# Keeping both split parts of three in four trunk weight tiles in DRAM

## The chip, the cores and the metric

The kernel runs on one core of a Trainium2 chip. The metric is the device time in microseconds (us) of one execution. Before the change the median of three runs is 1823.28 us (1819.3 to 1824.56). Five engines work side by side, each through its own list of instructions in order: TensorE (PE) for matrix products, VectorE (DVE), ScalarE (ACT) and GpSimd (POOL) for elementwise work, SyncE (SP), which here issues nearly all transfers between DRAM and the on-chip memory. They wait for each other through semaphores.

## The reference

One layer of a streaming encoder in float32, over 1024 prompt frames and 32 sample frames (1056 columns), width 1024. Shortened:

```
h = rms_norm(x, g_mix);  z = h @ w_in            # q k v, conv_h conv_B conv_C, two gates
a = window_attention(q, k, v) @ w_attn_out
bo = (cb * causal_conv3(cc * ch)) @ w_conv_out
x = x + (sigmoid(ga) * a + sigmoid(gb) * bo) @ w_mix_out
hc = rms_norm(x, g_cross)
x = x + memory_attention(hc @ w_cq) @ w_co
hm = rms_norm(x, g_mlp)
x = x + square(relu(hm @ w_up)) @ w_down
y = rms_norm(x, g_final)
```

`w_conv_out` and `w_mix_out` (called `w_mix` in the kernel) are 1024 x 1024, `w_cq` is 1024 x 256, `w_co` 256 x 1024, `w_up` 1024 x 4096.

## The kernel before

**Layout.** Activations lie transposed: 128 features on the partitions, frames along the columns. The 1056 columns are cut into three chunks of 384, 384 and 288. Features come in 8 blocks of 128. Each weight is cut into tiles of 128 x 1024 float32 (0.524 MB); such a tile makes one block of 128 outputs from 8 blocks of inputs (a tile of `w_co` makes four blocks from two).

**Split products.** To keep float32 accuracy with the faster matmul type, each operand is split into a rounded high part and a low part, the remainder. `gemm` (lines 170 to 177) runs three matmuls for each of 8 blocks: high x high (line 175), high weight x low activation (176), low weight x high activation (177): 24 matmuls a tile and chunk. The split of a weight tile is a cast on ACT (`wh<-wr`, line 119) and a subtraction on DVE (`wl<-wr,wh`, line 120).

**The order of weights.** `item` collects steps into a list, and `worder` the weight tiles that they need in this order. `next_w` keeps up to three tiles ready ahead (`LOOK = 2`). `issue_w` makes one ready: it fetches the raw tile into `wr` (two buffers, line 137), takes a high and a low buffer (`wh`, `wl`, three each), and splits. The buffers rotate, so a tile's high and low parts can be written only when TensorE has left the tile that was three before.

**Kept tiles.** The trunk runs once for each chunk: eight tiles of `w_conv_out` (`do_conv_out`), then eight of `w_mix` (`do_mix`). Cross-attention of a chunk (`cross_steps`: two tiles of `w_cq`, the scores and values, two of `w_co`) runs beside the trunk of the next chunk, one step after each trunk tile (`beside`). Cross-attention of chunk three runs beside the first eight tiles of `w_up` for chunks one and two; these eight then serve chunk three. So 28 tiles are used three times each. `kept` names those tiles (line 1274): the odd ones, 14 of 28. When such a tile is first used, its low part is stored to DRAM (line 154); in its two further uses the raw tile and the low part are loaded (lines 137 and 148) and only the cast is done (line 149). The other 14 are fetched and split at each use.

**Beside the tiles.** `do_conv_out` loads `t1` (line 786) and multiplies by a gate (line 790); line 791 adds on POOL. `do_mix` loads the input rows (line 801), adds them on DVE (line 805), and splits the scaled result (lines 255, 256). Cross-attention copies and adds its two halves (lines 918, 919), and splits (925 to 931) for `do_co` (943 to 945), whose result DVE adds in line 947. Lines 972 to 976 normalise rows for the up products, store them (973) and split them. Line 816 loads memory keys, line 828 splits memory values. Three accumulators (`acc`) rotate, so an addition on DVE that is late holds back TensorE.

**Order.** The program text gives dependencies and a rough order; a planner with a model of each engine's time lays down each engine's list before the run. SP's list is one of these: a load that waits for a buffer holds back all that SP issues behind it.

Of the kernel before, what the change touches and what calls it, by code (L numbers as in the profile page):

```python
# [10 lines left out]
F32 = mybir.dt.float32  # L11
# [7 lines left out]
P = 128  # L19
# [19 lines left out]
def hybrid_step(ctx: ExitStack, tc: tile.TileContext, io):  # L39
    nc = tc.nc  # L40
    act, dve, pool_e, pe, sp = nc.scalar, nc.vector, nc.gpsimd, nc.tensor, nc.sync
# [3 lines left out]
    def nm(s):  # L45
        uid[0] += 1
        return f"{s}_{uid[0]}"
# [15 lines left out]
    dram = ctx.enter_context(tc.tile_pool(name="dram", bufs=1, space=DRAM))  # L63
# [42 lines left out]
    plan, worder, kept = [], [], {}  # L106
# [11 lines left out]
    def split(hi, lo, src):  # L118
        act.copy(hi, src)  # L119
        dve.tensor_sub(lo, src, hi.bitcast(F32))  # L120

    def weight(key):
        name, *at = key
        if name in ("w_down", "w_sum"):
            q, j, t = at
            return (wsum_d if name == "w_sum" else io[name])[j, t, :, :, q].rearrange("i p c -> p i c")
        src = io[name]
        for j in at:
            src = src[j]
        return src  # L130

    fetched = []

    def fetch_w():
        raw = wp.tile([P, 1024], F32, tag="wr", bufs=2, name=nm("wr"))
        src = weight(worder[wpos[0] + len(fetched)])
        sp.dma_start(raw.rearrange("p (i c) -> p i c", i=4) if len(src.shape) == 3 else raw, src)
        fetched.append(raw)

    def issue_w():  # L140
        if not fetched:
            fetch_w()
        raw = fetched.pop(0)
        key = worder[wpos[0]]
        hi = wp.tile([P, 1024], F32R, tag="wh", name=nm("wh"))
        lo = wp.tile([P, 1024], F32R, tag="wl", name=nm("wl"))
        if kept.get(key) is not None:
            sp.dma_start(lo.bitcast(F32), kept[key])
            act.copy(hi, raw)
        else:  # L150
            split(hi, lo, raw)
            if key in kept:
                kept[key] = dram.tile([P, 1024], F32, name=nm("wl_d"))
                sp.dma_start(kept[key], lo.bitcast(F32))
        ready.append((worder[wpos[0]], (hi, lo)))
        wpos[0] += 1

    def next_w(key):
        while len(ready) <= LOOK and wpos[0] < len(worder) and worder[wpos[0]] is not STOP:
            issue_w()  # L160
        k, w = ready.pop(0)
        assert k == key, (k, key)
        return w
# [104 lines left out]
    def norm_x():  # L268
# [48 lines left out]
        with tc.manual_schedule(engines={mybir.EngineType.SP}):  # L317
            load_x()
        parts(0, range(1))
        issue_w()  # L320
        parts(0, range(1, NF))
        issue_w()
        issue_w()
        wk, wv = ready[0][1], (ready[1][1], ready[2][1])
# [91 lines left out]
    def do_K(pr, extras=()):  # L416
        def fn(w):
            kt = at_tile([P, NT], F32, "kt")
            ktt[pr] = kt
            for c, (o, n) in enumerate(CH):  # L420
                a = acc_tile([P, n])
                gemm(a, w, xg[c])
                dve.tensor_mul(kt[:, o : o + n], a, R[c])
                after(extras, c)
            sp.dma_start(io["o_k"][pr], kt[:, 896:])

        return fn
# [22 lines left out]
    def do_Q(kv, j, extras=()):  # L450
        def fn(w):
            for c, (o, n) in enumerate(CH):
                npr = min(n, NPR - o)
                if j == 0:
                    qs[kv, c] = at_tile([P, 4, npr], F32R, "QA" if c < 2 else "QB", 2 if c < 2 else 1)
                    if n > npr:
                        qs[kv, 3] = at_tile([P, 4, n - npr], F32R, "QC")
                a = acc_tile([P, n])
                gemm(a, w, xg[c])
                t = tmp(n)  # L460
                dve.scalar_tensor_tensor(t, a, 0.125, R[c], op0=ALU.mult, op1=ALU.mult)
                parts = [(qs[kv, c], slice(0, npr))]
                if n > npr:
                    parts.append((qs[kv, 3], slice(npr, n)))
                for q, s in parts:
                    for e in range(2):
                        own, other = slice(64 * e, 64 * e + 64), slice(64 - 64 * e, 128 - 64 * e)
                        h = 2 * j + e
                        act.copy(q[own, h], t[own, s])
                        dve.tensor_sub(q[other, h], t[own, s], q[own, h].bitcast(F32))  # L470
                after(extras, c)

        return fn
# [151 lines left out]
    def do_gate(f, extras=()):  # L625
        def fn(w):
            for c, (o, n) in enumerate(CH):
                a = acc_tile([P, n])
                gemm(a, w, xg[c])
                t = gate_slot(c, f)  # L630
                dve.tensor_mul(t, a, R[c])
                act.activation(t, t, AF.Sigmoid)
                sg[c][f] = t
                after(extras, c)

        return fn
# [21 lines left out]
    for i, h in enumerate(hosts):  # L658
# [9 lines left out]
        if h[0] == "Q":  # L668
            fn, key = do_Q(h[1], h[2], extras), qt(h[1], h[2])
        elif h[0] == "K":  # L670
            fn, key = do_K(h[1], extras), ("w_in", 8 + h[1])
        elif h[0] == "G":
            fn, key = do_gate(h[1], extras), ("w_in", 34 + h[1])
        else:
            fn, key = do_conv(*h, extras), conv_w(h[1], h[0])
# [577 lines left out]
    def beside(steps, fillers, late=()):  # L1253
        for i, filler in enumerate(fillers):
            item(*filler)
            for x in [x for at, x in late if at == i]:
                item(lambda x=x: x())
            if steps:
                kind, what = steps.pop(0)
                for x in what:  # L1260
                    if kind == "items":
                        item(*x)
                    else:
                        item(lambda x=x: x())
        return steps

    def trunk(c):
        return [(do_conv_out(c, f), ("w_conv_out", f)) for f in range(NF)] + [
            (do_mix(c, f), ("w_mix", f)) for f in range(NF)
        ]  # L1270

    up0 = lambda c: [do_up(j, c) for j in range(NF)]
    for name, n in (("w_conv_out", NF), ("w_mix", NF), ("w_cq", 2), ("w_co", 2), ("w_up", NF)):
        kept.update(((name, j), None) for j in range(1, n, 2))
    left = beside([], trunk(0))
    left = beside(cross_steps(0), trunk(1))

# [322 lines left out]
```

## Time and profile before

| | before |
|---|---|
| median of runs | 1823.28 us |
| profiled execution, its own time | 1822.32 us |
| its span, first to last instruction | 1820.5 us |
| PE / DVE / ACT / POOL busy | 1769.7 / 1110.2 / 757.0 / 531.4 us |
| mean granted TensorE clock | 0.99 |
| DMA, all queues | 293.35 MB, mean 161 GB/s |
| loads of kept low parts | 28 of 512 KB, median 4.8 us from issue to landing |
| stores of kept low parts | 14 of 512 KB, median 3.0 us |

A group row of the profile names source line, engine, operation, output<-input with buffer numbers left out, and a count. A row of stretches gives for each engine its busy time (with the count of instructions), then the granted TensorE clock, the share of time in which the 16 DMA engines were busy, and GB/s. In a timeline row the first two numbers are start and duration; a bracket gives the idle time of the engine before it and what ended it. The ends of matmuls are modelled, and PE, the bottleneck here, counts as busy while they overlap.

### The profile page before, as it was taken

The numbers are of one execution on the slowest core, as the hardware profiler recorded it, in microseconds if no ns is written. First come the engines' busy times: TensorE is split into PE (matmuls) and PEld (weight loads), VectorE is DVE, ScalarE is ACT, GpSimd is POOL, SyncE is SP. The second block draws the span as 40 slices with busy tenths as digits, with TensorE's granted clock in tenths as the row PEclk, the third lists the DMA queues.
The fourth block names the chain that finished last, engine by engine and source line by source line (L and its number), as shares of the span: only waits on it lengthen the run. The fifth ranks groups of instructions, "written<-read, shape, count | busy, mean of one in ns | idle before, by whom it ended". The sixth has DMA issues, their size and how long they took to land. (4 is left out here: it accounts for less than half of the span.)

```text
span 1820.5 us, 29893 instructions
## 1 busy us (share of the span) xinstructions
PE 1769.7 (97%) x11172; PEld 1750.3 (96%) x11172; DVE 1110.2 (61%) x2083; ACT 757.0 (42%) x1486; POOL 531.4 (29%) x597
## 2 busy tenths in 40 slices
PE   7899999999999999999999989999999999999997
PEld 7899999999999999999999979999999999999997
DVE  7886766757665222425666768667566676436663
ACT  7553544535335210423465755632222343324453
POOL 4554310110113333002515142376544300100111
PEclk9999999999999999999999999999999999999999
DMA  6454411211126455516756657654334597446573
GB/s 224 161 175 150 149 56 53 80 56 63 61 93 199 148 174 183 163 55 210 242 197 214 225 191 251 241 189 140 133 125 138 160 295 223 156 128 205 193 241 105
DMA packets 166305, 293.35 MB, mean 161 GB/s; under 512 B 16624, under 2 KB 128016, under 8 KB 166032
## 3 DMA queue, kind: packets, MB, share of 16 engines
q1 hardware_dynamic: 156944, 257.88, 42.9%
q0 software_dynamic: 9216, 33.56, 5.2%
q8 instruction: 88, 1.44, 0.4%
q14 instruction: 57, 0.47, 0.1%
HBM read 217.89 MB, written 73.48 MB: 160 GB/s over the span
## 5 line engine op out<-in xcount | busy, mean ns | idle before, releaser
L175 PE MATMUL acc<-X,wh 128*128 128x384 f32 (+1 forms) x1200 | 392.1, 327 | 11.3 <-ACT wh L119 8.3
L176 PE MATMUL acc<-X,wh 128*128 128x384 f32 (+1 forms) x1200 | 389.0, 324 | 3.9 <-DVE X L256 3.9
L177 PE MATMUL acc<-X,wl 128*128 128x384 f32 (+1 forms) x1200 | 388.1, 323 | 0.4 <-DVE wl L120 0.4
L119 ACT CAST wh<-wr 128x1024 fp32r<-128x1024 f32 x208 | 218.2, 1049 | 361.1 <-PE acc L176 177.0
L120 DVE TENSOR_TENSOR wl<-wr,wh 128x1024 fp32r<-128x1024 f32 x208 | 274.3, 1319 | 99.8 <-ACT wh L119 98.7
L175 PEld LDWEIGHTS acc<-X,wh 128*128 128x128 f32 x1200 | 227.4, 189 | 12.0 <-ACT wh L119 8.3
L176 PEld LDWEIGHTS acc<-X,wh 128*128 128x128 f32 x1200 | 227.5, 190 | 4.9 <-DVE X L256 4.2
L177 PEld LDWEIGHTS acc<-X,wl 128*128 128x128 f32 x1200 | 227.2, 189 | 1.0 <-DVE wl L120 0.9
L175 PE MATMUL acc<-Y,wh 128*128 128x384 f32 (+1 forms) x624 | 202.4, 325 | 0.7 <-DVE ct L1000 0.4
L177 PE MATMUL acc<-Y,wl 128*128 128x384 f32 (+1 forms) x624 | 201.9, 324 | 0.0
L176 PE MATMUL acc<-Y,wh 128*128 128x384 f32 (+1 forms) x624 | 201.7, 323 | 0.0
L252 POOL TENSOR_TENSOR xacc<-xacc,ct 128x384 f32<-128x384 f32 (+1 forms) x62 | 76.5, 1237 | 319.3 <-ACT ct L250 314.2
L175 PEld LDWEIGHTS acc<-Y,wh 128*128 128x128 f32 x624 | 117.0, 188 | 1.4 <-DVE ct L1000 0.6
L176 PEld LDWEIGHTS acc<-Y,wh 128*128 128x128 f32 x624 | 117.1, 188 | 0.0
L177 PEld LDWEIGHTS acc<-Y,wl 128*128 128x128 f32 x624 | 117.1, 188 | 0.0
L1363 PE MATMUL acc<-Y,wh 128*128 128x384 f32 (+1 forms) x352 | 113.2, 322 | 1.3 <-DVE lt L1145 0.7
L1364 PE MATMUL acc<-Y,wh 128*128 128x384 f32 (+1 forms) x352 | 113.3, 322 | 0.6 <-DVE Y L120 0.6
L1365 PE MATMUL acc<-Y,wl 128*128 128x384 f32 (+1 forms) x352 | 113.0, 321 | 0.0
L119 ACT CAST PTh<-pt 128x512 fp32r<-128x512 f32 (+3 forms) x94 | 46.2, 516 | 124.5 <-PE pt L550 117.1
L120 DVE TENSOR_TENSOR Y<-ct,Y 128x384 fp32r<-128x384 f32 (+1 forms) x128 | 66.2, 549 | 42.3 <-ACT Y L119 42.1
L119 ACT CAST Y<-ct 128x384 fp32r<-128x384 f32 (+1 forms) x128 | 58.8, 486 | 59.0 <-DMA ct<-b_d 14.9
L1004 POOL TENSOR_TENSOR ct<-ct 128x288 f32<-128x288 f32 (+1 forms) x48 | 44.8, 934 | 120.3 <-DVE ct L1000 49.8
(309 smaller groups left out, 4192.5 us busy)
## 6 DMA issues: line engine op xcount, KB each, us to landing
wr<-in_w_in SPq DMA_DIRECT2D x50, 512.0 KB, 3.4
wr<-in_w_up SPq DMA_DIRECT2D x48, 512.0 KB, 3.9
wr<-in_w_down SPq DMA_DIRECT2D x32, 512.0 KB, 3.7
wr<-wsum_d SPq DMA_DIRECT2D x32, 512.0 KB, 3.5
wl<-wl_d SPq DMA_DIRECT2D x28, 512.0 KB, 4.8
wr<-in_w_conv_out SPq DMA_DIRECT2D x24, 512.0 KB, 4.2
wr<-in_w_mix SPq DMA_DIRECT2D x24, 512.0 KB, 4.2
ct<-b_d SPq DMA_DIRECT2D x48, 192.0 KB, 4.4
```

Source lines behind the costliest of these rows:

```text
L119: act.copy(hi, src)
L120: dve.tensor_sub(lo, src, hi.bitcast(F32))
L175: pe.matmul(out, wh[:, a], hi, start=(k == 0), stop=False)
L176: pe.matmul(out, wh[:, a], lo, start=False, stop=False)
L177: pe.matmul(out, wl[:, a], hi, start=False, stop=(k == len(acts) - 1))
L252: pool_e.tensor_tensor(acc, acc, sq, op=ALU.add)
L1004: pool_e.tensor_tensor(h, t, t, op=ALU.mult)
L1363: pe.matmul(a, wh[:, s], hi, start=(start and k == 0), stop=False, skip_group_check=True)
L1364: pe.matmul(a, wh[:, s], lo, start=False, stop=False, skip_group_check=True)
L1365: pe.matmul(a, wl[:, s], hi, start=False, stop=(stop and k == len(acts) - 1), skip_group_check=True)
```

## The change

The kept tiles become those whose number is not a multiple of four: six of each eight and one of each two, 20 of 28. A kept tile's first use fetches and splits it as before, and stores both parts. Its later uses load both parts straight into the high and low buffers; the raw tile is not fetched then, and nothing is cast. A tile that isn't kept is fetched and split at every use, as before.

```diff
     def issue_w():
-        if not fetched:
-            fetch_w()
-        raw = fetched.pop(0)
         key = worder[wpos[0]]
         hi = wp.tile([P, 1024], F32R, tag="wh", name=nm("wh"))
         lo = wp.tile([P, 1024], F32R, tag="wl", name=nm("wl"))
         if kept.get(key) is not None:
-            sp.dma_start(lo.bitcast(F32), kept[key])
-            act.copy(hi, raw)
+            for x, d in zip((hi, lo), kept[key]):
+                sp.dma_start(x.bitcast(F32), d)
         else:
-            split(hi, lo, raw)
+            if not fetched:
+                fetch_w()
+            split(hi, lo, fetched.pop(0))
             if key in kept:
-                kept[key] = dram.tile([P, 1024], F32, name=nm("wl_d"))
-                sp.dma_start(kept[key], lo.bitcast(F32))
+                kept[key] = [dram.tile([P, 1024], F32, name=nm("w_d")) for _ in range(2)]
+                for x, d in zip((hi, lo), kept[key]):
+                    sp.dma_start(d, x.bitcast(F32))
...
     for name, n in (("w_conv_out", NF), ("w_mix", NF), ("w_cq", 2), ("w_co", 2), ("w_up", NF)):
-        kept.update(((name, j), None) for j in range(1, n, 2))
+        kept.update(((name, j), None) for j in range(n) if j % 4)
```

## The prediction

> **What bounds the kernel now.** I read the page's busy shares first, then stretches cut at the passes of the trunk, then who TensorE waited for, then single instructions around its largest gap.
>
> ```profile
> span 1820.5 us, 29893 instructions
> PE 1769.7 (97%) x11172; PEld 1750.3 (96%) x11172; DVE 1110.2 (61%) x2083; ACT 757.0 (42%) x1486; POOL 531.4 (29%) x597
> ```
>
> TensorE is busy for 97% of the span, so casts taken from ACT and DVE can only pay where TensorE stands still. The stretches are the first chunk's trunk, the second's beside cross-attention of the first, the third's, the first eight up tiles for chunks one and two, and the same tiles for chunk three; further rows cut the third closer and show two stretches outside the change.
>
> ```profile
> core 0: us, PE busy (x) PEld busy (x) DVE busy (x) ACT busy (x) POOL busy (x), PEclk, DMA share, GB/s
> 824.80:892.20 67.40, 67.40 (x388) 67.40 (x387) 42.57 (x56) 27.46 (x41) 28.11 (x18) 1.00 0.69 230
> 892.20:985.00 92.80, 92.41 (x546) 91.45 (x545) 59.87 (x106) 54.27 (x100) 35.48 (x29) 1.00 0.62 211
> 985.00:1080.00 95.00, 87.24 (x584) 83.72 (x584) 67.64 (x131) 58.83 (x114) 32.07 (x31) 0.96 0.64 214
> 1080.00:1160.00 80.00, 78.54 (x496) 77.46 (x494) 58.35 (x119) 44.38 (x98) 14.72 (x16) 1.00 0.68 227
> 1160.00:1200.00 40.00, 38.49 (x272) 37.79 (x272) 31.01 (x45) 22.43 (x38) 26.41 (x24) 1.00 0.84 296
> ...
> 1040.00:1060.00 20.00, 14.45 (x84) 12.11 (x82) 15.06 (x26) 11.25 (x21) 6.63 (x6) 0.94 0.71 238
> 1060.00:1080.00 20.00, 17.79 (x100) 16.68 (x101) 14.42 (x22) 10.68 (x18) 14.98 (x14) 0.89 0.49 155
> ...
> 1480.00:1500.00 20.00, 20.00 (x131) 20.00 (x130) 14.53 (x25) 9.12 (x17) 0.00 (x0) 1.00 0.95 319
> ```
>
> The first pass loses nothing, the second 0.4 us, the third 7.8, the last two 1.5 each: 11.1 us in all, and nearly all of the third's between 1040 and 1080. No other engine is full there. What TensorE waits for there:
>
> ```profile
> 1053.73 0.44 PE L943 MATMUL acc<-Y,wh 128*128 128x384 f32 x1 [1.45 <-DVE Gb L805]
> ...
> 1054.92 0.44 PE L943 MATMUL acc<-Y,wh 128*128 128x384 f32 x1 [0.41 <-ACT Y L925]
> 1056.05 0.45 PE L944 MATMUL acc<-Y,wh 128*128 128x384 f32 x1 [0.68 <-DVE Y L931]
> ...
> 1057.59 0.69 PE L943 MATMUL acc<-Y,wh 128*128 128x384 f32 x1 [0.92 <-DVE Ga L947]
> ...
> 1058.72 0.53 PE L943 MATMUL acc<-Y,wh 128*128 128x384 f32 x1
> 1059.04 0.53 PE L944 MATMUL acc<-Y,wh 128*128 128x384 f32 x1
> ...
> 1063.88 0.51 PE L945 MATMUL acc<-Y,wl 128*128 128x384 f32 x1
> ```
>
> It is the chain of small DVE and ACT steps around the output of cross-attention. After these gaps the matmuls of three outputs, 18 of them from 1057.59 to 1063.88, start 0.32 us apart (1058.72, 1059.04) where 0.173 is usual (seven steps from 870.17 to 871.38, further below): the granted clock has dropped.
>
> **The change: counts.**
>
> ```profile
> L119 ACT CAST wh<-wr x208: 1027/1049/1058, 7.2 to 1794.3; 128x1024 fp32r<-128x1024 f32 x104
> L120 DVE TENSOR_TENSOR wl<-wr,wh x208: 1208/1225/2317, 8.2 to 1795.4; 128x1024 fp32r<-128x1024 f32 x104
> L149 ACT CAST wh<-wr x28: 1032/1049/1057, 891.6 to 1189.0; 128x1024 fp32r<-128x1024 f32 x28
> ...
> L148 SPq DMA_DIRECT2D wl<-wl_d x28: 319/327/1205, 890.3 to 1191.3; - x28
> L154 SPq DMA_DIRECT2D wl_d<-wl x14: 319/326/381, 815.8 to 1111.1; - x14
> ...
> DMA to landing us min/median/max: 2.9/3.9/6.9
> ```
>
> The tiles kept go from 14 of 28 to 20 (six of each eight, one of each two). Each is used twice more. So the 28 casts of line 149 go, and 12 further tile uses lose their cast and their subtraction: 40 x 1.049 = 42.0 us of ACT, 12 x 1.225 = 14.7 us of DVE. Loads: 28 low parts become 80 loads of both parts, 40 raw loads go, net +12; stores go from 14 to 40, +26. Each moves 0.524 MB (128 x 1024 x 4 bytes), so 38 more carry 19.9 MB. By pass: 16 stores; 4 loads and 2 stores; 4 loads; 2 loads and 8 stores; 2 loads.
>
> **What is gained.** Most of the 42 us lie beside a TensorE that does not wait (passes one and two show 0.4 us), and are worth nothing. In the gap of the third pass the removed steps stand directly ahead of the late ones:
>
> ```profile
> 1050.12 1.21 DVE L120 TENSOR_TENSOR wl<-wr,wh 128x1024 fp32r<-128x1024 f32 x1
> ...
> 1053.23 0.44 DVE L805 TENSOR_TENSOR Gb<-acc,ct 128x288 f32<-128x288 f32 x1
> ...
> 1055.44 0.55 DVE L931 TENSOR_TENSOR Y<-tO,h 64x384 fp32r<-64x384 f32 x1 [1.30 <-ACT h L930]
> ...
> 1053.29 1.05 ACT L149 CAST wh<-wr 128x1024 fp32r<-128x1024 f32 x1
> 1054.36 0.51 ACT L925 CAST Y<-tO 64x384 fp32r<-64x384 f32 x1
> ```
>
> The subtraction at 1050.12 is that of tile six of `w_mix`, which will be kept; without it the DVE steps up to line 805 move up by 1.2 us. The cast at 1053.29, of the second `w_co` tile, sits ahead of lines 925 and 930, for which DVE then waits; without it they move up by 1.05. That shortens the three waits (1.45, 0.41, 0.68) by about 2.2 us. What is late next is line 947, which shares DVE with the steps for the third chunk (0.92), and line 805 where its input rows come late. The 18 matmuls at 0.32 us cost 18 x 0.147 = 2.6 us; I count half, 1.3, because part of the idle time stays. The last two stretches lose 1.5 us each, with eight and six casts fewer; I take a third of it, 1.0 (bounds 0 and 3.0). Gains: 4.5 us, between 0 and 13.4 (7.8 + 2.6 + 3.0).
>
> The Trainium skill, "TensorE: Matmul & The Clock Gate", Part 1, says that TensorE falls to half its clock after one idle window of about 3.4 us and returns after one busy one. The spacing here, 0.32 against 0.173, agrees. By that rule the 2.6 us come whole or not at all, so the sum would be 1.3 us lower or higher.
>
> **What is added, first pass.** 16 stores more are 8.39 MB in 67.4 us, 124 GB/s on top of 230: 354. The row at 1480 moves 319 at a share of 0.95, which puts full engines at 336. So the demand is over what the engines move by 18 GB/s, 1.2 MB, or 3.6 us of backlog by the end of the pass. The stores themselves may be late, since a buffer returns only three tiles later. What cannot be late are the raw loads behind them on SP's queue.
>
> ```profile
> 868.32 0.41 ACT L119 CAST mkh<-mkr 128x256 fp32r<-128x256 f32 x1 [3.26 <-DMA mkr<-in_cmem_k]
> 868.63 1.05 ACT L119 CAST wh<-wr 128x1024 fp32r<-128x1024 f32 x1
> ...
> 869.71 1.23 DVE L120 TENSOR_TENSOR wl<-wr,wh 128x1024 fp32r<-128x1024 f32 x1
> ...
> 870.17 0.33 PE L177 MATMUL acc<-M,wl 128*128 128x384 f32 x1
> ...
> 871.38 0.33 PE L175 MATMUL acc<-M,wh 128*128 128x384 f32 x1
> ...
> L175 PE MATMUL acc<-M,wh x192: 290/334/421, 858.9 to 1076.8; 128*128 128x384 f32 x128, 128*128 128x288 f32 x64
> ```
>
> Mixing starts at 858.9 and a tile lasts 24 x 0.173 = 4.2 us, so its fourth tile starts at 871.4; its split ended at 870.94. The slack is 0.4 us, because ACT stood 3.26 us behind a load of memory keys. One pair of stores (1.05 MB, 3.1 us at 336 GB/s) ahead of such a load can cost 2.7 us. Bounds: 0 (TensorE shows 20.00 of 20 us at a share of 0.95) and 3.6 - 0.4 + 2.6 of clock = 5.8. I take 1.5, nearer the row at 0.95.
>
> The Trainium skill, "DMA: Bandwidth & Descriptors", section "Measured", gives a load stream of one core 425 GB/s. By it 354 would leave room and this term would be zero: a forecast 1.5 us lower. No row here reaches that rate, and loads, stores and short rows are mixed in it.
>
> **What is added, later passes.** Demand becomes 211 + 34 = 245 GB/s, 214 + 22 = 236, 227 + 66 = 293 and 296 + 26 = 322, all under 336. Only the first 40 us of the fourth stretch, which carry its eight stores, come near full: 227 + 105 = 332. A kept tile now needs no ACT or DVE, but both loads can start only when TensorE has left the buffers of three tiles before. From there two tiles pass: 8.4 us with 384 columns, two times 24 x 0.13 = 6.2 with 288 (0.13 is 0.173 by the columns). The low part alone lands in 3.9 us, at most 6.9; the second load adds 0.524 MB, 1.6 us: 5.5, at most 8.5. So the median fits and the slowest are 2.3 us late; bounds 0 and, for three such tiles, 6.9. I take 0.
>
> Behind such a waiting load on SP stand the loads of `ct` for lines 790 and 805, and the stores of normalised rows.
>
> ```profile
> SPq L137 <- DVE wl L120: 121.1, 34, 11.1
> ...
> SPq L148 <- PE acc L177: 27.7, 14, 4.0
> ...
>   DMA ct<-in_x: 23.1, 9
> ```
>
> From 780 to 1200 SP waits 27.7 us for TensorE before 28 loads. With 40 kept uses instead of 28 that becomes about 40, but 40 of 84 raw loads, with 121.1 us behind the subtraction, go. I put this at nothing; if it is wrong, the nine waits of line 805 for its input rows (23.1 us of DVE in all) grow by up to 1.6 each, 14 us of DVE. 38 issues at 0.33 us are 12.5 us of SP, hidden since SP mostly waits.
>
> The order on each engine is laid by a planner, and other tiles mean another order. No row prices that; what TensorE loses from 1200 to 1440, with other work, is the nearest:
>
> ```profile
> 1200.00:1440.00 240.00, 237.50 (x1484) 236.95 (x1483) 152.33 (x190) 62.56 (x77) 134.75 (x109) 0.99 0.40 131
> ```
>
> 2.5 us, either way; taken as 0.
>
> **The sum.** -4.5 + 1.5 = -3.0. The profiled execution took 1822.3 us (its span and 1.8 around it), 1.0 under the median of the runs, 1823.3. So 1819.3 for an execution like it, **1820** as a median.
>
> **Rivals.**
> *The whole gap closes.* If the DVE queue gets ahead, line 805 is not late, the clock stays up and the third pass keeps pace. For it: the gap is one chain with the removed steps in it. Against: part of line 805's lateness is a load (23.1 us), which nothing here makes earlier. -13.4 + 1.5 = -12: 1811.
> *The DMA engines fill, and it is slower.* Place: the mixing half of the first pass. Load requests queue behind pairs of stores, splits finish after TensorE is ready, and the clock drops. It decides once a raw load is 0.4 us late on the fourth mixing tile. Price: 5.8 there, 2.3 for one pair of loads at its slowest in the last stretch, less 1 of relief that later input rows leave: +7, 1830. For it: 354 against 336. Against: 0.95 with no gap.
> *Hidden anyway.* Relief and delays both fall beside TensorE's work, or cancel (a late pair, 2.3): 1823.
>
> **How the numbers follow.** A measurement of this kernel tells about 0.3%, 5.5 us, from no change. The forecast has 0.37 (0.14 of it beyond 5.5 us, since its gain may reach 6 to 8; 0.23 within), the closed gap 0.24, full DMA engines 0.28 (0.27 slower), hidden 0.11 (0.09 within, 0.02 slower). Faster 0.14 + 0.24 = 0.38, the same 0.33, slower 0.29. The range takes in 1811 less 3 of planner's order, and 1830 with 4 more for late pairs: 1808 to 1834. The forecast's own range is 1814 to 1825.
>
> **What would show it.** Right: no group of casts on line 149; 80 loads and 40 stores of kept tiles; ACT about 42 us less, DVE about 15; the shortfall from 1040 to 1080 down from 7.8 us by 2 to 4; the first pass near a DMA share of 1.0 with under 2 us lost. Wrong: TensorE waiting on weights in the first pass, on a load of `wh` or `wl` itself in later ones, or line 805's wait for input rows well over 23 us; or a changed idle time after 1200, where nothing was edited.

## The result, and the profile after

The changed kernel takes 1830.64 us (median of 6 runs, 1827.6 to 1832.68), the kernel before beside it on the same chip 1821.85 us (6 runs, 1819.07 to 1824.56). The ratio is **1.0053, 95% interval 1.004 to 1.0067**: slower by 0.5%, where 1820 and a small gain were forecast. The profiled spans are 1820.5 and 1828.8 us.

The page's busy shares of the changed kernel, then its median landing times (KB each, us):

```profile
PE 1769.3 (97%) x11172; PEld 1751.4 (96%) x11172; DVE 1096.0 (60%) x2071; ACT 717.5 (39%) x1446; POOL 519.0 (28%) x597
...
wh<-w_d SPq DMA_DIRECT2D x40, 512.0 KB, 4.8
wl<-w_d SPq DMA_DIRECT2D x40, 512.0 KB, 5.9
...
w_d<-wh SPq DMA_DIRECT2D x20, 512.0 KB, 4.2
w_d<-wl SPq DMA_DIRECT2D x20, 512.0 KB, 4.3
```

The change does what it says: 80 loads and 40 stores, ACT 39.5 us less (757.0 to 717.5), DVE 14.2 less. TensorE's work is the same, so the 8.2 us are time in which it stood still or ran slowly. The same stretches as in the prediction, for the changed kernel:

```profile
core 0: us, PE busy (x) PEld busy (x) DVE busy (x) ACT busy (x) POOL busy (x), PEclk, DMA share, GB/s
824.80:892.20 67.40, 67.40 (x389) 67.40 (x389) 42.58 (x51) 25.79 (x37) 17.78 (x16) 1.00 0.92 330
892.20:985.00 92.80, 87.23 (x508) 86.51 (x507) 52.87 (x99) 40.00 (x84) 30.51 (x26) 0.96 0.67 236
...
1040.00:1060.00 20.00, 19.44 (x147) 19.13 (x145) 17.49 (x32) 11.43 (x25) 4.83 (x5) 1.00 0.76 264
1060.00:1080.00 20.00, 15.94 (x74) 14.22 (x75) 15.43 (x24) 8.30 (x17) 9.47 (x11) 0.83 0.53 185
880.00:890.00 10.00, 10.00 (x60) 10.00 (x59) 6.47 (x7) 3.51 (x6) 4.54 (x4) 1.00 1.00 364
895.00:900.00 5.00, 2.90 (x17) 2.58 (x15) 1.54 (x2) 1.45 (x2) 0.52 (x1) 1.00 0.99 384
900.00:905.00 5.00, 1.80 (x6) 1.81 (x7) 2.06 (x4) 0.92 (x2) 1.70 (x2) 0.50 0.72 244
905.00:910.00 5.00, 5.00 (x25) 5.00 (x24) 2.31 (x5) 1.72 (x4) 2.18 (x3) 0.81 0.34 106
```

TensorE loses nothing in the first pass, as before, although the DMA engines are busy for 0.92 of it (0.69 before) and all of the time from 880 to 890. Just behind its end 5.3 us go, from 895 to 905, and the granted clock is 0.50, then 0.81 in the last two rows. The two rows of the third pass hold later work than the same rows before did, since this kernel is some 6 to 10 us behind there. The 184 matmuls that ran from 1040 to 1080 in the kernel before stand between 1049.80 and 1085.70 here; 4.6 us of TensorE are lost among them, where it was 7.8:

```profile
1049.80:1085.70 35.90, 31.29 (x184) 29.29 (x183) 28.36 (x44) 16.71 (x31) 18.22 (x19) 0.90 0.66 231
```

To see where the difference comes from, the same matmuls were looked up in both traces and their starts subtracted. One of these places, line 880 (scores of cross-attention) with its first and last start, in the kernel before:

```profile
L880 PE MATMUL sc<-mkh,Y x36: 274/279/285, 918.3 to 1143.8; 128*128 128x256 f32 x36
```

And in the changed one:

```profile
L880 PE MATMUL sc<-mkh,Y x36: 274/279/385, 926.9 to 1152.3; 128*128 128x256 f32 x36
```

The shift between the traces, place by place (us from the start of the span):

| place | before | after | shift | change of it |
|---|---|---|---|---|
| first mixing matmul | 858.88 | 859.73 | +0.85 | +0.85 |
| first score of cross-attention | 918.28 | 926.93 | +8.65 | **+7.80** |
| last mixing matmul of line 176 | 1076.96 | 1082.67 | +5.71 | -2.94 |
| last product of `w_co` (line 943) | 1166.15 | 1173.01 | +6.86 | +1.15 |
| last up product (line 1070) | 1461.44 | 1465.37 | +3.93 | -2.93 |
| first down product (line 1363) | 1462.86 | 1472.13 | +9.27 | **+5.34** |
| end of the span | 1820.55 | 1828.78 | +8.23 | -1.04 |

So two places take 13.1 us and two give back 5.9. The table's first line is what is left of the wait for the very first weight, which ended at 10.3 us where it was 8.3; it varies by about 2 us among the kernels below though their code there is one.

**The first place: 7.8 us where the first pass hands over to the second.** TensorE's largest idle time there, in the timeline of the changed kernel:

```profile
903.20 0.69 PE L175 MATMUL acc<-Y,wh 128*128 128x384 f32 x1 [5.30 <-DVE Gb L805]
```

DVE's timeline there:

```profile
898.88 1.23 DVE L120 TENSOR_TENSOR wl<-wr,wh 128x1024 fp32r<-128x1024 f32 x1 [2.93 <-ACT wh L119]
902.58 0.56 DVE L805 TENSOR_TENSOR Gb<-acc,ct 128x384 f32<-128x384 f32 x1 [2.47 <-DMA ct<-in_x]
```

ACT's, some 15 us earlier, with the split of a raw mixing tile:

```profile
885.23 1.05 ACT L119 CAST wh<-wr 128x1024 fp32r<-128x1024 f32 x1 [3.95 <-DMA wr<-in_w_mix]
```

And the loads that SP issued in between (start, time on SP):

```profile
891.17 0.53 SPq L146 DMA_DIRECT2D wh<-w_d  x1
891.79 0.38 SPq L146 DMA_DIRECT2D wl<-w_d  x1
892.26 0.38 SPq L137 DMA_DIRECT2D wr<-in_w_cq  x1
893.05 0.32 SPq L146 DMA_DIRECT2D wh<-w_d  x1
893.46 0.62 SPq L146 DMA_DIRECT2D wl<-w_d  x1
894.27 0.81 SPq L801 DMA_DIRECT2D ct<-in_x  x1
```

Read backwards: TensorE waits for an accumulator that line 805 reads last. Line 805 waits for its input rows. These were issued at 894.27, behind two pairs of kept parts (2.1 MB, the first loads of the second pass) and a raw load, and were there by 902.58, 8.3 us later. In the kernel before, the rows for the same mixing tile, number six counting from 0, were issued at 887.55 and were there by 892.07. SP's timeline, then DVE's, of the kernel before:

```profile
887.55 0.79 SPq L801 DMA_DIRECT2D ct<-in_x  x1
```

```profile
892.07 0.56 DVE L805 TENSOR_TENSOR Gb<-acc,ct 128x384 f32<-128x384 f32 x1 [1.05 <-DMA ct<-in_x]
```

They are issued later, by 6.7 us, and land 3.8 us more slowly. Of the 7.8 us, 5.30 and a wait of 0.27 are idle time; the clock takes about 1.9 (half of the 1.80 us worked from 900 to 905, and 0.19 of the next five); 0.4 is not accounted for.

**The second place: 5.3 us at the first down product.** TensorE's timeline in the kernel before:

```profile
1462.86 0.41 PE L1363 MATMUL acc<-Y,wh 128*128 128x384 f32 x1 [0.74 <-DVE lt L1145]
```

And in the changed one:

```profile
1472.13 0.66 PE L1363 MATMUL acc<-Y,wh 128*128 128x384 f32 x1 [6.07 <-DVE lt L1159]
```

TensorE's products and DVE's steps stand in the same order in both kernels here. What differs is whose accumulator the first down product takes: before, the one that line 1145 reads last; now the one that line 1159 reads last, 5.3 us further down DVE's list. None of the edited code runs there. It came with the schedule that was laid for the changed program; why the rotation came out this way, no run shows.

### The profile page after: what moved, and what is told of

It reads as the page before. It is cut to its first block, busy times and chain, and to the rows that moved or that the text cites. A ratio compares the mean times of both kernels' runs of the same rounds, so it can differ in the third digit from the quotient of the medians.

```text
span 1828.8 us, 29884 instructions
## 1 busy us (share of the span) xinstructions
PE 1769.3 (97%) x11172; PEld 1751.4 (96%) x11172; DVE 1096.0 (60%) x2071; ACT 717.5 (39%) x1446; POOL 519.0 (28%) x597
## 2 busy tenths in 40 slices
DMA packets 171777, 313.27 MB, mean 171 GB/s; under 512 B 17232, under 2 KB 128624, under 8 KB 171504
## 4 chain that ended last, share of the span: by engine, by line
PE 84%; DMA 7%; DVE 4%; issue 2%; ACT 2%; POOL 1%; SPq 0%; POOLq 0%; DVEq 0%; ACTq 0%
PE acc L175 16%; PE acc L176 16%; PE acc L177 16%; PE acc L1363 5%; PE acc L1364 5%; PE acc L1365 5%; PE acc L1072 3%; PE acc L1071 3%; PE acc L1070 3%; PE pt L550 1%; PE pa L176 1%; PE pa L175 1%; PE pa L177 1%; DMA wr<-in_w_mix 1%; ACT wh L119 1%
## 5 line engine op out<-in xcount | busy, mean ns | idle before, releaser
L175 PE MATMUL acc<-X,wh 128*128 128x384 f32 (+1 forms) x1200 | 391.8, 327 | 13.4 <-ACT wh L119 10.3
L119 ACT CAST wh<-wr 128x1024 fp32r<-128x1024 f32 x196 | 205.8, 1050 | 386.0 <-PE acc L176 188.8
L120 DVE TENSOR_TENSOR wl<-wr,wh 128x1024 fp32r<-128x1024 f32 x196 | 259.7, 1325 | 116.4 <-ACT wh L119 115.1
L175 PEld LDWEIGHTS acc<-X,wh 128*128 128x128 f32 x1200 | 227.1, 189 | 14.1 <-ACT wh L119 10.3
```

Of the source, the lines that this page charges most:

```text
L175: pe.matmul(out, wh[:, a], hi, start=(k == 0), stop=False)
```

## The experiments

Each is one edit, beside the kernel before on the same chip. "Boundary loss" is the shift, against the profiled kernel before, of the first score of cross-attention less that of the first mixing matmul: 7.8 us in the changed kernel. It also counts a change of order: 345 matmuls start in between in the kernel before, in the changed one and wherever no other count is given, and each one more or fewer is 0.173 us that is neither loss nor gain. Where an edit adds lines, line 805 of the kernel before is 813 (fetching rows early) or 809 (stores alone), and 1070 is 1078. The first theory, A, was that the input rows of the last mixing tile are held up behind a load on SP's queue; B, that the full DMA engines as such cost the time.

**Input rows one tile early.** On the changed kernel, all the rest as it is:

```diff
+    def fetch_rows(c, f):
+        xt = tmp(CH[c][1])
+        sp.dma_start(xt, io[f"x{c}"][:, f])
+        return xt
...
-            xt = tmp(n)
-            sp.dma_start(xt, io[f"x{c}"][:, f])
+            xt = rows_in.pop((c, f)) if (c, f) in rows_in else fetch_rows(c, f)
+            if f + 1 < NF:
+                rows_in[c, f + 1] = fetch_rows(c, f + 1)
```

> The changed kernel, but each mixing tile also asks for the input rows (line 801) of the next one, so that the rows of the last mixing tile of the first chunk stand ahead of the memory-key loads and of the raw load of w_conv_out on SP's queue. The bytes are the same, 313 MB. Theory A (place on SP's queue: those rows were issued at 900.5, behind a raw load that waited for its buffer): the wait of 5.3 us at 903 and its clock dip go, 1822 to 1824. Theory B (the DMA engines are full, share 0.92 to 1.0 from 825 to 900): the bytes are as late as before, the wait moves elsewhere, 1829 to 1832.

Measured: 1816.69 us, ratio 0.9979 (0.9967 to 0.999); boundary loss -0.3 us, but with 333 matmuls in between: the twelve fewer are 2.1 us, so about 1.7 is lost. The bytes are the same, and the DMA engines are as full, as stretches of this kernel show:

```profile
880.00:900.00 20.00, 18.96 (x109) 18.15 (x109) 10.29 (x19) 7.50 (x11) 7.10 (x7) 1.00 1.00 358
895.00:900.00 5.00, 5.00 (x32) 4.84 (x31) 2.81 (x8) 2.94 (x4) 0.38 (x1) 1.00 1.03 405
```

SP's timeline has the rows asked for earlier:

```profile
880.59 0.38 SPq L801 DMA_DIRECT2D ct<-in_x  x1
884.53 0.41 SPq L801 DMA_DIRECT2D ct<-in_x  x1
```

Line 813 no longer waits for a load at all. The 1.04 us that TensorE still loses from 880 to 900 are two waits for the split of a weight tile, 0.46 us and this one:

```profile
892.74 0.44 PE L177 MATMUL acc<-Y,wl 128*128 128x384 f32 x1 [0.58 <-DVE wl L120]
```

So full engines with early rows cost 1.0 us of idle time, where they cost 7.8 with late ones. The wait at the first down product is gone too: the planner laid another order, and 0.5 us pass there from the last up product. This makes the change a gain, and the last run repeats it.

**The stores taken away.** Only the first kept tile is stored, and every kept tile then loads that one; the other 38 stores are left out, and later passes multiply with the wrong weights.

```diff
+            first = [d for d in kept.values() if d]
-            if key in kept:
+            if key in kept and first:
+                kept[key] = first[0]
+            elif key in kept:
```

> The changed kernel without 38 of its 40 stores: all kept tiles load the two parts that the first kept tile stored, so the later passes compute with wrong weights. The loads are as many as in the changed kernel. Theory B: with about 8.4 MB less than before in the first pass its share falls from 0.92 to about 0.45, no wait at its end: 1820 to 1822, and from 1815 if the casts saved are worth 3 to 5 us. Theory A: what counts is where the rows of line 801 stand; without stores they stand ahead of that raw load, so also 1820 to 1822. It tells stores (with what they do to the order) from loads of pairs: if it stays at 1828 or more, the pairs of loads are the cause.

Measured: 1815.92 us, ratio 0.9976 (0.9963 to 0.9988); boundary loss 0.0. The stretch of the first pass:

```profile
824.80:892.20 67.40, 67.40 (x387) 67.40 (x386) 47.50 (x56) 26.16 (x40) 26.16 (x20) 1.00 0.61 198
```

Without the stores' bytes (198 GB/s where there were 330) the same pairs of loads cost nothing at the boundary, and this kernel is 0.24% faster than the one before. It changes two things, though: with fewer stores on SP's list, tile six's rows were also issued at 881.33, ahead of every pair. So it does not tell full engines from late rows.

**Both parts of the same 14 tiles as before.** `for j in range(1, n, 2)` in the changed kernel.

> Both parts kept, but of the 14 odd tiles alone: 28 stores, 56 loads of parts, 56 raw loads. 8 stores more in the first pass than the kernel before, 16 fewer... that is 16 of the changed kernel's 24. The rows of the last mixing tile stand ahead of the w_cq load on SP's queue. Theory A: no wait at the end of the first pass, 1819 to 1823. Theory B: demand of the first pass 230 + 62 = 292 GB/s, share about 0.85: little or no wait as well, 1820 to 1824. Should it be near 1830, pairs of loads or the later passes are to blame.

Measured: 1825.1 us, ratio 1.0027 (1.0017 to 1.0037); boundary loss 4.9. Here TensorE waits for a kept part itself:

```profile
900.24 0.41 PE L175 MATMUL acc<-Y,wh 128*128 128x384 f32 x1 [2.08 <-DMA wh<-w_d]
```

Fewer tiles lessen the loss and do not remove it. Here it is a pair that is late, and not the rows.

**The stores alone.** The kernel before, which also writes the parts that the changed one stores: 40 stores in all, 26 of them never read.

```diff
+            if key in more and more[key]:
+                for x in (hi, lo)[: more[key]]:
+                    sp.dma_start(dram.tile([P, 1024], F32, name=nm("w_d")), x.bitcast(F32))
+                more[key] = 0
...
+        more.update({(name, j): 2 - j % 2 for j in range(n) if j % 4})
```

> The kernel before (odd low parts kept, casts as before) with the same 40 stores in the first uses as the changed kernel; 26 of them are never read. It has the changed kernel's load in the first pass and none of its saved casts or loaded pairs. Theory B: the wait at the end of the first pass appears, 5 to 8 us: 1827 to 1830. Theory A: its last rows of line 801 stand behind a raw load of w_cq and two memory-key loads, less far back than in the changed kernel: 1822 to 1826.

Measured: 1824.35 us, ratio 1.0023 (1.0012 to 1.0034); boundary loss 2.7, with 347 matmuls. A stretch of this kernel:

```profile
880.00:890.00 10.00, 10.00 (x59) 9.85 (x58) 6.41 (x7) 3.31 (x5) 3.93 (x4) 1.00 1.02 356
```

And TensorE's waits behind it, in its timeline:

```profile
894.09 0.42 PE L179 MATMUL acc<-Y,wh 128*128 128x384 f32 x1 [0.93 <-DVE Gb L809]
899.35 0.42 PE L179 MATMUL acc<-Y,wh 128*128 128x384 f32 x1 [0.83 <-ACT wh L119]
```

SP issued tile six's rows, and DVE added them:

```profile
893.25 0.42 SPq L805 DMA_DIRECT2D ct<-in_x  x1
```

```profile
898.65 0.56 DVE L809 TENSOR_TENSOR Gb<-acc,ct 128x384 f32<-128x384 f32 x1 [1.67 <-DMA ct<-in_x]
```

So the late issue (887.55 in the kernel before, 894.27 in the changed one) comes with the stores alone. Without pairs ahead of them the rows then took 5.3 us to land, where they took 8.3, and the engines were as full: a share of 0.99 from issue to landing in both. In the kernel before the share is 1.01 there and the rows took 4.4 us. So it is the loads ahead of the rows that make the landing slow, and not the share. Stores alone give 2.7, pairs without the stores (the run before last) 0.0, both together 7.8: the loss is no sum of two prices.

**Rows of the last mixing tile alone.** As the first experiment, with `if (c, f) == (0, NF - 2):`, so only tile seven's rows of chunk one are early.

> The changed kernel with one load asked for earlier: the input rows of the last mixing tile of the first chunk, by one tile. On SP's queue this load then stands before two memory-key loads and the raw load of w_conv_out instead of behind them; the rest of SP's list around it stays as it was. Theory A (place on SP's queue): the wait of 5.3 us and the clock dip behind it, together 7.8 us by the time cross-attention of the first chunk starts, go: 1822 to 1824. Theory B (full DMA engines): one load of 192 KB doesn't change their load, and less than 2 us are won: 1828 to 1831.

Measured: 1831.94 us, ratio 1.0062 (1.0045 to 1.0078); boundary loss 8.4. Nothing is cured. SP's timeline in this kernel:

```profile
895.73 0.83 SPq L801 DMA_DIRECT2D ct<-in_x  x2
```

DVE's:

```profile
903.53 1.17 DVE L813 TENSOR_TENSOR Gb<-acc,ct 128x384 f32<-128x384 f32 x2 [2.91 <-DMA ct<-in_x]
```

And TensorE's:

```profile
904.14 0.69 PE L175 MATMUL acc<-Y,wh 128*128 128x384 f32 x1 [5.73 <-DVE Gb L813]
```

Theory A named the wrong rows and falls in that form. Those of tile six are the late ones; tile seven's were only asked for together with them. Theory C takes its place: tile six's rows, issued late, behind two pairs of loads, into full engines.

**Rows of tiles five and six.** `if (c, f) in ((0, NF - 4), (0, NF - 3)):`

> The changed kernel with the input rows of mixing tiles five and six of the first chunk (counted from zero) asked for one tile earlier; then tile six's rows stand before the two pairs of part loads on SP's queue, tile seven's still behind them. Theory C (tile six's rows were issued at 894.3 right behind two pairs, 2.1 MB, and landed 8.3 us later; the wait at 903 is theirs): the larger part of the 7.8 us goes, 1823 to 1826. If the rows' place is not it, and only fewer bytes would help: 1829 to 1832, as when tile seven's rows alone were moved.

Measured: 1827.66 us, ratio 1.0033 (1.0021 to 1.0044); boundary loss 7.1, with 354 matmuls. Tile six's addition is now in time (893.19 instead of 902.58), and the stall has moved one tile on. DVE's timeline:

```profile
903.05 1.23 DVE L120 TENSOR_TENSOR wl<-wr,wh 128x1024 fp32r<-128x1024 f32 x1 [3.92 <-ACT wh L119]
904.19 0.55 DVE L813 TENSOR_TENSOR Gb<-acc,ct 128x384 f32<-128x384 f32 x1
```

TensorE's:

```profile
904.80 0.44 PE L175 MATMUL acc<-Y,wh 128*128 128x384 f32 x1 [2.69 <-DVE Gb L813]
```

Two things hold it. Tile seven's rows now have the place that tile six's had, issued at 894.27 behind two pairs, and took 8.4 us to land, until 902.7. And its addition stands in DVE's list behind a subtraction, whose cast waits 4.11 us for TensorE to leave an older weight tile; by these times about 1.4 of the 2.69 us are the subtraction's. Of the 7.1 us, 1.6 are order (nine matmuls more), 3.3 idle time (0.60 at 898.00 for a kept part, and 2.69), 1.7 the clock (0.66 from 905 to 910), and 0.5 are open. So C is right about which load was late and why, and not about what its cure is worth: the next tile's rows are late in the same way.

**Fewer pairs at that place.** The changed kernel without `w_mix` tiles five, six and seven among the kept: `for j in (5, 6, 7): kept.pop(("w_mix", j))`.

> The changed kernel without tiles five, six and seven of w_mix among the kept: 6 stores (3.1 MB, 9 us of full DMA engines) fewer between 876 and 890, and in the two later passes 12 part loads fewer, 6 raw loads, 6 casts and 6 subtractions more. Theory C with engines filled by stores: the share in 880 to 890 falls from 1.00 to about 0.6, the rows land in time: 1821 to 1825. If the pairs at the start of the second pass are enough to delay the rows: 1827 to 1831.

Measured: 1821.66 us, ratio 0.9994 (0.9982 to 1.0006); boundary loss 0.2. A stretch of this kernel:

```profile
880.00:890.00 10.00, 10.00 (x60) 10.00 (x59) 9.86 (x10) 4.81 (x7) 7.30 (x5) 1.00 0.73 231
```

With 6 stores less just before the boundary the engines are not full there (0.73), and TensorE waits for nothing from 870 to 926. As in the run with two stores, tile six's rows were issued early without an edit of theirs, at 887.58 and ahead of the pairs, so again less traffic and earlier issue come together.

**Both cures.** Rows early, and those three tiles not kept.

> The same without tiles five to seven of w_mix kept, and all input rows one tile early. If the first pass still costs the rows-early variant something (it lost 1.0 us there between 880 and 900), this one is 0 to 1.5 us faster than it; if the casts and subtractions that come back in the later passes weigh more, 1 to 3 us slower: 1815 to 1820.

Measured: 1821.76 us, ratio 0.9994 (0.9985 to 1.0003); boundary loss 0. That is a miss: the cures do not add. Rows early had already taken all but 1.0 us of the boundary loss. From the first score to the last mixing matmul this kernel gains 2.4 us on the kernel before; with the three tiles kept it was 2.9, and 4.0 in the repeat, and 2.1 us more in both, because twelve matmuls that stand ahead of the first score elsewhere come after it there. In the third pass TensorE waits 3.80 us for line 813 here (at 1056.11), 2.31 us with rows early alone (at 1053.60). The steps that came back would fit that; no run takes it apart. From the last up product to the end it takes 361.2 us, 359.1 in the kernel before and 358.7 and 357.4 with rows early alone; why, the runs do not show.

**Controls.** The kernel before with rows early; the kernel before with its low parts kept for the 20 tiles (`j % 4`, casts stay); rows early in the changed kernel without the six tiles of `w_up`.

> The kernel before with the input rows asked for one tile earlier, as in the run that was faster than before. If that run's gain (0.21%) belongs to the earlier rows alone, this one shows it too: 1816 to 1819. If it belongs to the casts saved by the kept pairs, this one stays within 1820 to 1823, save for what line 805 waits less (its 23 us of DVE waits lie mostly beside TensorE's work; I expect up to 2 us).

> The kernel before with 20 instead of 14 tiles kept, low parts alone: 6 stores and 12 loads more, 12 subtractions less, casts as before. The rows of the last mixing tile stand just behind a low-part load, as in the kernel before. No wait at the end of the first pass; saved subtractions are worth up to 1.2 us in the third pass: 1819 to 1823. If more stored tiles as such cost time, 1825 or more.

> The faster variant (kept pairs, rows early) without the eight w_up tiles among the kept: 12 stores fewer and 24 part loads fewer, 24 raw loads instead, and 12 casts and 12 subtractions more than it in the last two stretches of the trunk. If the stores and pair loads there cost TensorE time (the share was 0.83 and 0.92), it is 1 to 4 us faster: 1813 to 1816. If the casts and subtractions saved there are the larger thing, it is 2 to 4 us slower: 1818 to 1821.

Measured: 0.9994 (0.9984 to 1.0005), 1.0008 (0.9995 to 1.002) and 1.0016 (1.0003 to 1.0029); medians 1819.88, 1823.44 and 1823.57 us. So early rows show no gain by themselves, and 12 subtractions less (14.7 us of DVE) none either: what pays is loading both parts, with the casts gone, and of the runs with all stores in place only those with all 20 tiles and all rows early show it. In the third the boundary loss is small too (-0.8 with 333 matmuls; 0.64 us of idle time), but without the pairs of `w_up` the gain is gone as well. From the last product of `w_co` to the last up product it takes 297.5 us, with those pairs 293.0; part of its time is lost only after that, though, so the step is not settled by this run.

**The faster version again.** The first experiment, run again beside its own runs of the kernel before.

> The rows-early variant once more, to see its gain over the kernel before on another chip or day: 0.997 to 0.999 of it, 1815 to 1819.

Measured: 1815.93 us, **ratio 0.9965 (0.9952 to 0.9978)**; boundary loss -0.8 with 333 matmuls, 0.64 us of idle time. It beats both kernels.

## Why the prediction was wrong

**What bounds the kernel, and the counts: right.** 80 loads, 40 stores, no cast on line 149, 19.9 MB more (293.35 to 313.27), ACT 39.5 us less for 42.0 forecast, DVE 14.2 for 14.7.

**The gain: right in size, not in its way.** 4.5 us were forecast. The third pass gained 2.9 (forecast 3.5, 1.3 of it the clock's); rows early give 0.9979 and 0.9965, and the run without stores 0.9976, 4 to 6 us. But the three named waits did not shorten by 2.2 together. In TensorE's timeline after:

```profile
1061.15 0.45 PE L943 MATMUL acc<-Y,wh 128*128 128x384 f32 x1 [1.71 <-DVE Gb L805]
...
1063.93 0.69 PE L944 MATMUL acc<-Y,wh 128*128 128x384 f32 x1 [1.23 <-DVE Y L931]
```

They were 1.45 and 0.68. The clock fell for as long as before, so its 1.3 did not come. Before, then after:

```profile
1057.40:1064.20 6.80, 5.70 (x15) 4.68 (x16) 4.38 (x9) 2.52 (x6) 2.35 (x3) 0.50 0.41 152
```

```profile
1063.90:1070.70 6.80, 6.12 (x18) 5.61 (x19) 4.26 (x8) 1.57 (x3) 1.47 (x2) 0.50 0.27 93
```

What went were other gaps, which the prediction had not quoted, the largest 1.68 us at 1048.02, behind line 919. So the size agrees in part by luck. Taking a cast out of a list moved the whole order, not the two steps behind it. "The last two stretches", 1.0 forecast, gave a loss of 1.2 by the last product of `w_co` instead; the up products after it gained 2.9, with no row of mine for it. The seven kernels that store and load six pairs of `w_up` take 290.7 to 293.0 us there, the kernel before 295.3, the one with four 294.5, and those without any 294.9 to 297.5; but the kernel without stores, which loads the pairs too, takes 296.1. What makes it is open.

**The first-pass term: the step that failed.** It was taken as 1.5 between 0 and 5.8; measured, 7.8, over the upper bound. Full engines with early rows lose 1.0 us of idle time, 0.6 in the repeat; the rest of the 7.8 is the late rows, what stands behind them on the engines' lists, and the clock. Three things in the term were wrong.
- The rate was worked out from a mean, 354 GB/s wanted against 336 to be had. In the trace the pass moves 330 on the mean and 364 to 384 where it is full, up to 405 with rows early, and that faster kernel loses no more than that 1.0. So 336 was too low as a ceiling, and the comparison of means was not the question. The Trainium skill, "DMA: Bandwidth & Descriptors", section "Measured", with 425 GB/s for a load stream, was the nearer ceiling: the best five us here, with loads and stores mixed, show 405. By it the term would have been zero, which is further from 7.8 than what I took: a ceiling in GB/s doesn't give the lateness of one load.
- What cannot be late was said to be "the raw loads behind them". One was late (3.95 us on ACT at 885.23), and TensorE did not wait for it. By the order of SP's list it made what follows there late; no run takes that step apart.
- The place was not the first pass at all but its hand-over, where the stores of one pass and the pairs of the next meet. The later passes were costed on their own means (245 GB/s, "all under 336"), and the meeting was in no term.

**"I put this at nothing".** The prediction named the loads of `ct` for line 805 behind pairs on SP, and gave them no cost on the path, because SP's waits even out. They do: DVE waits 15.2 us for those rows in all, 23.1 before. The sum fell, and one of the nine waits, 2.47 us, cost TensorE 5.3 us and its clock. The condition given was a pair that waits for TensorE on SP; in fact the pairs ahead waited 0.5 us there, and the rows were late because of their late place in the list and the 2.1 MB ahead of them in full engines.

**Later passes: right, the median by luck.** Pairs landed in 5.4 us at the median and 8.5 at most, as forecast (5.5 and 8.5), and TensorE waited 1.1 us for parts in all. But the 3.9 us that the forecast began with is the median of the 28 loads and the 14 stores together; the loads alone took 4.8, which with 1.6 more would have given 6.4.

**Planner's order: taken as 0, within 2.5.** After 1166 it made -2.9, +5.3 and -1.0 us, +1.4 in sum, but the one wait of 6.07 us is twice that bound. The same wait stands in the two kernels with one and two early rows (6.09 and 6.08), and in none of those with all rows early (0.5 us from the last up product to the first down product). That sets part of the difference between the changed kernel and the fastest one. I made no kernel that changes this wait alone.

**The rivals.** "The DMA engines fill" gave the time, 1830, and the mechanism in part: full engines, a late load, the clock. Its place (the fourth mixing tile), its trigger (0.4 us) and its price (5.8) were not these, and 5.3 us of the measured loss are not in it. Its time came out right, by luck, from two terms, of which it had one. "The whole gap closes" did not come: 4.6 us of the third pass's gap from 1040 to 1080 stay. "Hidden anyway" holds for the second pass alone: behind its start the shift stays at 8.65 until 970, the third pass gains.

## What to carry to other kernels

Look for the place where the traffic of two stages meets, and there ask of each small load that is needed soon what is issued ahead of it; a mean rate over a stage says little. If such loads (here 192 KB of rows for every tile) are asked for one tile earlier, full engines cost 1.0 us here instead of 7.8: that one edit, with the order that the planner laid for it, turned 0.5% slower into 0.2 to 0.35% faster. And where a planner or a rotation of buffers lays the order, compare the starts of the same instructions at several places, for a difference may lie where nothing was edited. Count the instructions between two such places as well, since a change of order looks like a loss or a gain.

## What was not expected of the hardware

- **Throughput and lateness part.** With rows early, a share of 1.00 with 358 GB/s from 880 to 900, up to 405 in five us, went by with 1.04 us of TensorE's time lost. In the changed kernel, at 384, one 192 KB load took 8.3 us from issue to landing, where the rows of line 801 have a median of 4.7.
- **The clock fell after shorter idle times than I had reckoned.** In the kernel with rows five and six early, 2.69 us idle before 904.80 are followed by a clock of 0.50 from 906 to 908; in the kernel with the same 14 tiles, 2.08 us before 900.24 (and 0.59 more before 901.41) are followed by 0.50 from 902 to 904. The rule that the prediction took from the Trainium skill ("TensorE: Matmul & The Clock Gate", Part 1: half the clock after one idle window of about 3.4 us) would by its words have let both pass; the measurement decides. In both the drop begins 1 to 2 us after TensorE has started again. Stretches of two us, the kernel with rows five and six:

```profile
906.00:908.00 2.00, 2.00 (x8) 2.00 (x7) 0.54 (x2) 0.00 (x0) 0.96 (x1) 0.50 0.98 307
```

And the one with the same 14 tiles:

```profile
902.00:904.00 2.00, 2.00 (x8) 2.00 (x8) 1.32 (x3) 0.80 (x2) 0.00 (x0) 0.50 0.21 47
```

The kernel before already shows it: half the clock for 6.8 us from 1057.4, with no single idle time of TensorE above 1.68 us in the 10 us ahead. So where the prediction says that the spacing agrees, the half agrees and the 3.4 us do not.

- **One edit's stall uncovers the next within a tile.** With tile six's rows in time, TensorE stalled 2.69 us on tile seven's addition, whose rows took 8.4 us and which stood behind a subtraction; only the kernels with all rows early, or with stores taken away, cleared both.
